# The four rotation products of a state-space scan block on VectorE instead of GpSimd

## The chip, the core and the metric

The kernel runs on one core of a Trainium2 chip. A core has engines that each work through a queue of their own in order: TensorE (PE; its weight loads are shown as PEld), VectorE (DVE), ScalarE (ACT), GpSimd (POOL), and SyncE (SP), which issues the DMA transfers. They work side by side and wait for one another through semaphores. The metric is the device time of one execution in microseconds (us); lower is better. For the kernel before there are three timed runs and one further execution under the profiler.

## The reference

Two layers of a hybrid block over 1024 latent and 256 context tokens of width 1024. Each layer makes one input projection whose columns go to three mixers, differential attention, a state-space scan in both directions (S5), and Fourier mixing, then an output projection and a squared-ReLU MLP. The change lies in the scan, which in the reference is

```
bu_re = jnp.einsum('blgp,gnp->blgn', uf, bb_re)
bu_im = jnp.einsum('blgp,gnp->blgn', uf, bb_im)
...
_, _, s_re, s_im = lax.associative_scan(_affine_combine, (a_re, a_im, bu_re, bu_im), axis=1)
...
y = einsum(s_re, c_re) - einsum(s_im, c_im)          # s5_readout
```

a complex linear recurrence s[t] = a s[t-1] + b u[t] for each of 16 groups with 64 states, in both directions, followed by a gelu and a gated unit (GLU).

## The kernel before

The scan is done over chunks of 8 tokens: 160 chunks for 1280 tokens, two groups at a time, so that a layer has 8 blocks. The complex rotation in the recurrence is taken out by multiplying with precomputed cosines and sines (the tile CS), so that a real scan with the magnitude rho remains, and is put back after it. A block of `states` thus runs, in this order:

- PE: transposes of the inputs (L997, L998), then the products with the block's matrices (L1005); ACT copies the result into VS (L1006 to L1008)
- four instructions of 128x640 float32 elements on POOL: T1 = VS cos, T2 = VS sin (L1012, L1013) ahead of the scan, T1 = Z cos, T2 = Z sin (L1020, L1021) behind it
- DVE: the sums of the first pair (L1014, L1015, 128x320), four scans (L1018, 128x160), the sums of the second pair, shifted by one chunk (L1027 to L1031)
- `readout`, one block later: PE multiplies the states with the output matrices (L1039, L1040, L1041), ACT and DVE make the gelu (L1044 to L1049), and after every fourth block SP writes eight transfers to HD (L1052)

There are 16 blocks in all, hence 64 such products.

The scan is not a stage of its own. It is a generator, `mixers`, of which `run` takes a step after each tile of the input projection. The projection (`in_proj`) multiplies 24 matmuls per tile of 128 tokens (L584; for the last column block, V, twice 12, L611). The weights of a column block are split into a rounded part and a rest by ACT and DVE (L159, L160) before PE can use them. A tile of queries or keys is then normalised and rotated in `qk_post` on DVE (L534 to L545); its inverse square root is a 128x8 power on POOL (L133), and PE transposes the result (L551).

What follows is attention: the loads of keys from KD (L633, tiles s_t) and of queries from QD (L641), the scores (L649), and, taken in steps between them, `glu`, which loads the scan's result from HD (L1076) and multiplies it on PE (L1085).

The order of instructions on each engine is not written out by hand. The tile framework simulates the program when it is built (`schedule_with_timeline_sim=True`) and fixes each queue by the times that it works out, so that a change of engine moves other instructions too. Tiles come from pools with a fixed number of buffers; the scan's work tiles are in `bg`, 7 buffers here, and PSUM has four banks for the projection and four for the rest.

Of the kernel before, what the change touches and what calls it, by code (L numbers as in the profile page):

```python
# [18 lines left out]
ALU = mybir.AluOpType  # L19
# [48 lines left out]
class Block:  # L68
# [890 lines left out]
    def ssm(self, l):  # L959
        nc, io = self.nc, self.io  # L960
        last = l == DEPTH - 1
        c0 = 32 if last else 0
        work = self.tl('kv', [128, 2, 8, NCH])
        HH = work[:, 0]
        ut = self.tl('kv', [128, 2560])
        U = ut[:, 0:2048].rearrange('c (j f) -> c j f', j=8)
        for h in range(2):
            nc.sync.dma_start(U[:, :, h * 128:h * 128 + 128],
                              self.UF[0:SEQ, h * 128:h * 128 + 128].rearrange('(c j) f -> c j f', j=8))

        def x1(i, part=128):
            return work[0:part, 1, 2 * i:2 * i + 2]

        def load(b):
            PA = self.tl('pa', [128, 2, 5, 128])
            nc.sync.dma_start(PA[:, :, 1:5], self.PD[l][b])
            kw = self.KW[l][b]
            for g in range(2):
                w = kw[:, g, 0:128]
                w = bass.AP(w.tensor, w.offset, [(SP, 8), *w.ap])  # L980
                nc.sync.dma_start(PA[:, g, 0], w)
            CS = self.bg([128, 2, 2, NCH])
            nc.sync.dma_start(CS, self.CD[l][b])
            return PA, CS

        def states(b, PA, CS):
            g0 = b * 2
            uc = ut[0:32, 2304:2560].rearrange('c (j f) -> c j f', j=8)
            nc.sync.dma_start(uc, self.UF[SEQ:TOK, g0 * 16:g0 * 16 + 32].rearrange('(j c) f -> c j f', c=32))
            UC = x1(2, 32)[:, :, 0:128]  # L990
            UM = ut[:, 2048:2304].rearrange('c (g f) -> c g f', g=2)
            for dst, src in ((UC, uc), (UM, U[:, :, g0 * 16:g0 * 16 + 32])):
                for g in range(2):
                    nc.scalar.copy(dst[:, g].rearrange('c (j q) -> c j q', j=8), src[:, :, g * 16:g * 16 + 16])
            p = self.pf((128, 2, NCH))
            for g in range(2):
                nc.tensor.transpose(p[:, g, 0:32], UC[:, g], self.idn[0:32, 0:32])  # L997
                nc.tensor.transpose(p[:, g, 32:160], UM[:, g], self.idn)  # L998
            UT = x1(b % 2)
            nc.scalar.copy(UT, p)  # L1000
            VS = self.bg([128, 2, 2, NCH])
            for g in range(2):
                p = self.pf((128, 2, NCH))
                for j in range(2):
                    nc.tensor.matmul(p[:, j], PA[:, g, 1 + j], UT[:, g], start=True, stop=True)  # L1005
                nc.scalar.copy(VS[0:64, :, g], p[0:64])  # L1006
                nc.scalar.copy(VS[64:128, :, g, 0:32], p[64:128, :, 0:32][:, :, ::-1])
                nc.scalar.copy(VS[64:128, :, g, 32:160], p[64:128, :, 32:160][:, :, ::-1])  # L1008
            cos = CS[:, 0].unsqueeze(1).to_broadcast([128, 2, 2, NCH])
            sin = CS[:, 1].unsqueeze(1).to_broadcast([128, 2, 2, NCH])  # L1010
            T1, T2, Z = (self.bg([128, 2, 2, NCH]) for _ in range(3))
            nc.gpsimd.tensor_tensor(T1, VS, cos, ALU.mult)  # L1012
            nc.gpsimd.tensor_tensor(T2, VS, sin, ALU.mult)  # L1013
            nc.vector.tensor_tensor(VS[:, 0], T1[:, 0], T2[:, 1], ALU.add)  # L1014
            nc.vector.tensor_tensor(VS[:, 1], T1[:, 1], T2[:, 0], ALU.subtract)  # L1015
            for j in range(2):
                for g in range(2):
                    nc.vector.tensor_tensor_scan(Z[:, j, g], self.rho[:, l * 16 + g0 + g:l * 16 + g0 + g + 1].to_broadcast([128, NCH]),  # L1018
                                                 VS[:, j, g], 0.0, ALU.mult, ALU.add)
            nc.gpsimd.tensor_tensor(T1, Z, cos, ALU.mult)  # L1020
            nc.gpsimd.tensor_tensor(T2, Z, sin, ALU.mult)  # L1021
            S = VS
            nc.vector.memset(S[0:64, :, :, 0:1], 0.0)
            nc.vector.memset(S[64:128, :, :, 31:32], 0.0)
            for j, op in enumerate((ALU.subtract, ALU.add)):
                a, c = T1[:, j], T2[:, 1 - j]
                nc.vector.tensor_tensor(S[0:64, j, :, 1:160], a[0:64, :, 0:159], c[0:64, :, 0:159], op)  # L1027
                if not last:
                    nc.vector.tensor_tensor(S[64:128, j, :, 0:31], a[64:128, :, 0:31][:, :, ::-1],
                                            c[64:128, :, 0:31][:, :, ::-1], op)  # L1030
                nc.vector.tensor_tensor(S[64:128, j, :, 32:160], a[64:128, :, 31:159][:, :, ::-1],  # L1031
                                        c[64:128, :, 31:159][:, :, ::-1], op)
            return PA, UT, S

        def readout(b, PA, UT, S):
            g0 = b * 2
            y = self.pf((128, 2, NCH))
            for g in range(2):
                nc.tensor.matmul(y[:, g, c0:], PA[:, g, 0], UT[:, g, c0:], start=True, stop=False)  # L1039
                nc.tensor.matmul(y[:, g, c0:], PA[:, g, 3], S[:, 0, g, c0:], start=False, stop=False)  # L1040
                nc.tensor.matmul(y[:, g, c0:], PA[:, g, 4], S[:, 1, g, c0:], start=False, stop=True)  # L1041
            yv = y[:, :, c0:]
            sq, y4 = (x1(2 + i)[:, :, c0:] for i in range(2))
            nc.scalar.activation(y4, yv, AF.Copy, scale=0.25)  # L1044
            nc.scalar.activation(sq, yv, AF.Square)
            nc.vector.tensor_scalar(sq, sq, 0.044715, 1.0, ALU.mult, ALU.add)
            nc.vector.tensor_tensor(sq, sq, y4, ALU.mult)
            nc.scalar.activation(sq, sq, AF.Tanh, scale=4.0 * math.sqrt(2.0 / math.pi))
            nc.vector.scalar_tensor_tensor(HH[:, g0 % 8:g0 % 8 + 2, c0:], sq, 1.0, y4, ALU.add, ALU.mult)  # L1049
            if b % 4 == 3:  # L1050
                for i in range(8):
                    nc.sync.dma_start(self.HD[b // 4 * 8:b // 4 * 8 + 8, :, i, c0:].rearrange('g q c -> q g c'),  # L1052
                                      HH[i * 16:i * 16 + 16, :, c0:])


        prev, nxt = None, load(0)
        yield
        for b in range(9):
            cur = (b, states(b, *nxt)) if b < 8 else None
            yield  # L1060
            if prev is not None:
                readout(prev[0], *prev[1])
            if b < 7:
                nxt = load(b + 1)
            if b:
                yield
            prev = cur
# [370 lines left out]
```

## Time and profile before

| | us |
|---|---|
| timed runs | 3080.57, 3086.21, 3086.28 |
| their median | 3086.21 |
| the profiled execution | 3082.04 |
| its span, first to last instruction | 3080.3 |
| PE busy in the span | 2948.4 (96%) |
| DVE busy | 1980.6 (64%) |
| ACT busy | 1074.5 (35%) |
| POOL busy | 590.7 (19%) |

The span is the time from the first to the last instruction of the profiled execution; 1.7 us lie around it. Busy times are unions over an engine's instructions. The shares are averages over stages: the blocks of the scan run from 268 to 440 us of the span in layer 0 and from 1890 to 2066 us in layer 1.

### The profile page before, as it was taken

Reading aid. Unit: us, or ns where it says so; the run is one execution under the profiler, and the core shown is the slowest. Engines: PE = TensorE matmul, PEld = TensorE weight load, DVE = VectorE, ACT = ScalarE, POOL = GpSimd, SP = SyncE. Lnnn points to the kernel's source line nnn. Section 1 sums busy time; section 2 is a strip of 40 time slices with the busy share of each in tenths; the row PEclk is TensorE's granted clock in tenths of the full one; section 3 lists DMA queues with packets and bytes.
Section 4 is the critical chain, followed back from the end, with each engine's and each line's share of the span. In section 5 each row is a group of like instructions: output and inputs, shape, how many; then the busy total and the mean of one; then the engine's idle time right before and its main releaser. Section 6 shows DMA issues by size and latency. Waiting matters only on the chain.

```text
span 3080.3 us, 41053 instructions
## 1 busy us (share of the span) xinstructions
PE 2948.4 (96%) x15309; PEld 2417.2 (78%) x15309; DVE 1980.6 (64%) x3546; ACT 1074.5 (35%) x2379; POOL 590.7 (19%) x515
## 2 busy tenths in 40 slices
PE   6899989999999999999999999989999999999999
PEld 3567777668888888888888877768889888888887
DVE  7867856666567677676545557959866555455444
ACT  5224436666331121121222243427864222211222
POOL 0644510000100000000266123526631000000000
PEclk9899999999999999999999999999999999999999
DMA  8345473435122232231222044571241111111111
GB/s 301 111 147 163 157 199 102 129 110 159 47 63 88 74 98 76 83 96 42 72 81 82 32 154 142 156 171 51 66 141 42 52 45 55 48 49 42 55 49 65
DMA packets 280852, 299.93 MB, mean 97 GB/s; under 512 B 47159, under 2 KB 191949, under 8 KB 280653
## 3 DMA queue, kind: packets, MB, share of 16 engines
q1 hardware_dynamic: 280652, 297.31, 31.8%
q8 instruction: 120, 1.97, 0.3%
q14 instruction: 80, 0.65, 0.1%
HBM read 229.31 MB, written 67.93 MB: 96 GB/s over the span
## 4 chain that ended last, share of the span: by engine, by line
PE 78%; DVE 8%; DMA 4%; issue 2%; ACT 2%; POOL 1%; SPq 0%; DVEq 0%; POOLq 0%; ACTq 0%
PE b_t L1241 26%; PE b_t L1264 25%; PE b_t L1208 7%; PE b_t L584 4%; PE b_t L695 4%; PE s_t L649 3%; PE b_t L417 2%; PE b_t L611 2%; PE b_t L691 1%; DVE mx L663 1%; DMA qs_t<-QD 1%; DMA s_t<-KD 1%; PE f_t L1124 1%; ACT s_t L665 1%; PE b_t L649 1%
## 5 line engine op out<-in xcount | busy, mean ns | idle before, releaser
L1264 PE MATMUL b_t<-hid_t,w_t 128*128 128x512 f32 (+1 forms) x3840 | 809.2, 370 | 0.0
L1241 PE MATMUL b_t<-s_t,w_t 128*128 128x512 f32 (+1 forms) x3840 | 800.4, 369 | 0.0
L1264 PEld LDWEIGHTS b_t<-hid_t,w_t 128*128 128x128 f32 x3840 | 669.7, 189 | 121.7 <-issue 1.9
L1241 PEld LDWEIGHTS b_t<-s_t,w_t 128*128 128x128 f32 x3840 | 669.1, 189 | 121.2 <-issue 1.1
L1266 DVE SCALAR_TENSOR_TENSOR kv_t<-b_t,mod,kv_t 128x512 f32<-128x512 f32 (+1 forms) x640 | 439.5, 694 | 240.2 <-PE b_t L1264 239.6
L159 ACT CAST w_t<-r_t 128x512 fp32r<-128x512 f32 x336 | 194.8, 619 | 797.3 <-PE b_t L1264 528.9
L584 PE MATMUL b_t<-w_t,s_t 128*128 128x512 f32 (+1 forms) x1392 | 356.7, 411 | 17.9 <-ACT s_t L474 6.0
L160 DVE TENSOR_TENSOR w_t<-r_t,w_t 128x512 fp32r<-128x512 f32 x328 | 230.8, 732 | 208.1 <-ACT w_t L159 207.7
L584 PEld LDWEIGHTS b_t<-w_t,s_t 128*128 128x128 f32 x1392 | 266.7, 198 | 81.7 <-issue 6.8
L133 POOL TENSOR_TENSOR sm<-sm,mhalf 128x8 f32<-128x8 f32 (+3 forms) x66 | 104.0, 1575 | 598.3 <-DVE sm L702 234.0
L1245 DVE TENSOR_TENSOR t_t<-b_t,t_t 128x512 f32<-128x512 f32 x160 | 101.3, 633 | 143.3 <-ACT t_t L1244 143.1
L892 POOL TENSOR_TENSOR bg_t<-pt_t,bw_t 128x256 f32<-128x256 f32 x56 | 42.8, 765 | 740.2 <-DMA bw_t<-BD 662.3
L695 PE MATMUL b_t<-kv_t,kv_t 128*128 128x128 f32 x1312 | 178.8, 281 | 3.0 <-ACT kv_t L692 2.8
L695 PEld LDWEIGHTS b_t<-kv_t,kv_t 128*128 128x128 f32 x1312 | 164.7, 194 | 16.7 <-issue 7.8
L663 DVE TENSOR_REDUCE mx<-s_t 128x1 f32<-128x1024 f32 x128 | 155.0, 1219 | 29.7 <-PE s_t L649 29.1
L1244 ACT ACTIVATE t_t<-b_t 128x512 f32<-128x512 f32 x160 | 88.4, 552 | 216.2 <-PE b_t L1241 216.2
L159 ACT CAST hid_t<-t_t 128x512 fp32r<-128x512 f32 x160 | 92.4, 578 | 204.1 <-DVE t_t L1245 204.0
L665 ACT ACTIVATE s_t<-s_t,mx 128x1024 f32<-128x1024 f32 x128 | 143.7, 1123 | 38.0 <-DVE mx L664 31.1
L160 DVE TENSOR_TENSOR hid_t<-t_t,hid_t 128x512 fp32r<-128x512 f32 x160 | 106.7, 667 | 66.2 <-ACT hid_t L159 66.2
L378 DVE SCALAR_TENSOR_TENSOR ac_t<-bg_t,vc,ac_t 128x512 f32<-128x512 f32 x168 | 118.9, 744 | 33.8 <-DMA bg_t<-in_w_mod_dram 33.6
L649 PE MATMUL s_t<-s_t,qs_t 128*128 128x512 f32 x448 | 128.2, 412 | 8.5 <-ACT s_t L665 5.5
L611 PE MATMUL b_t<-w_t,s_t 128*128 128x512 f32 x480 | 115.8, 395 | 6.6 <-DVE w_t L160 3.4
(332 smaller groups left out, 3550.5 us busy)
## 6 DMA issues: line engine op xcount, KB each, us to landing
r_t<-in_w_ff_dram SPq DMA_DIRECT2D x256, 256.0 KB
bg_t<-in_w_mod_dram SPq DMA_DIRECT2D x96, 256.0 KB
r_t<-in_w_in_dram SPq DMA_DIRECT2D x64, 256.0 KB
qs_t<-QD SPq DMA_DIRECT2D x64, 256.0 KB
XD<-kv_t SPq DMA_DIRECT2D x16, 640.0 KB
KD<-t_t SPq DMA_DIRECT2D x40, 256.0 KB
s_t<-KD SPq DMA_DIRECT2D x32, 320.0 KB
QD<-t_t SPq DMA_DIRECT2D x36, 256.0 KB
```

What stands on the lines that cost most here:

```text
L159: self.nc.scalar.copy(h, raw)
L160: (eng or self.nc.vector).tensor_tensor(l, raw, h, ALU.subtract)
L584: nc.tensor.matmul(p[:, :cols], a[:, ts], W[k][:, b, :cols], start=(n == 0), stop=(n == 23))
L611: nc.tensor.matmul(p, a[:, ts], W[k][:, b], start=(n == 0), stop=(n == 11))
L649: nc.tensor.matmul(dst, QS[e][:, m, h], ST[h][m][:, a:b], start=(e == 0), stop=(e == 1))
L663: nc.vector.tensor_reduce(mx[:, m, 1:2], S, AX.X, ALU.max, negate=True)
L665: nc.scalar.activation(PR[m][:, 0:SEQ], S, AF.Exp, bias=mx[:, m, 0:1], accum_out=sm[:, m, 1:2])
L695: nc.tensor.matmul(o, WT[:, kt * 128:(kt + 1) * 128], V[kt // 5][:, kt % 5, h * 128:(h + 1) * 128], start=(c == 0), stop=(c == len(ks) - 1))
L1208: nc.tensor.matmul(p[:, :w], W[c][a][:, k], b[k][:, s:s + w], start=(n == 0), stop=(n == 23))
L1241: nc.tensor.matmul(p[:, :w], W[a][:, k], b[k][:, s:s + w], start=(q == 0), stop=(q == 23))
L1264: nc.tensor.matmul(p[:, :w], W[a][:, cs], hid[b][:, s:s + w], start=(q == 0), stop=(q == n - 1))
L1266: nc.vector.scalar_tensor_tensor(xs, p[:, :w], self.mod[l][:, 40 + c, g // 2:g // 2 + 1], xs, ALU.mult, ALU.add)
```

## The change

The four products of a block are issued to DVE instead of POOL. Nothing else in the source differs, and the line numbers stay.

```
             T1, T2, Z = (self.bg([128, 2, 2, NCH]) for _ in range(3))
-            nc.gpsimd.tensor_tensor(T1, VS, cos, ALU.mult)
-            nc.gpsimd.tensor_tensor(T2, VS, sin, ALU.mult)
+            nc.vector.tensor_tensor(T1, VS, cos, ALU.mult)
+            nc.vector.tensor_tensor(T2, VS, sin, ALU.mult)
...
-            nc.gpsimd.tensor_tensor(T1, Z, cos, ALU.mult)
-            nc.gpsimd.tensor_tensor(T2, Z, sin, ALU.mult)
+            nc.vector.tensor_tensor(T1, Z, cos, ALU.mult)
+            nc.vector.tensor_tensor(T2, Z, sin, ALU.mult)
```

POOL loses 64 instructions and DVE gains 64, and the simulated order of PE, DVE, ACT and SP changes around them. First DVE, in the first scan block of layer 0; sm, t_t and qk_t belong to `qk_post`, w_t to the weights of the next column block, bg_t to the scan.

```order
 L535 TENSOR_SCALAR sm_2459<-sm_2459 128x8
+L1012 TENSOR_TENSOR bg_t_2408<-bg_t_2395,bg_t_2334 128x640
+L1013 TENSOR_TENSOR bg_t_2409<-bg_t_2395,bg_t_2334 128x640
 L160 TENSOR_TENSOR t_t_2472<-b_t_2466,t_t_2471 128x512
 L160 TENSOR_TENSOR w_t_2545<-r_t_2543,w_t_2545 128x512
 L545 TENSOR_TENSOR qk_t_2454<-qk_t_2454,sm_2460 128x512
+L1014 TENSOR_TENSOR bg_t_2395<-bg_t_2408,bg_t_2409 128x320
+L1015 TENSOR_TENSOR bg_t_2395<-bg_t_2408,bg_t_2409 128x320
 L160 TENSOR_TENSOR w_t_2550<-r_t_2548,w_t_2550 128x512
 L160 TENSOR_TENSOR w_t_2555<-r_t_2553,w_t_2555 128x512
-L1014 TENSOR_TENSOR bg_t_2395<-bg_t_2408,bg_t_2409 128x320
-L1015 TENSOR_TENSOR bg_t_2395<-bg_t_2408,bg_t_2409 128x320
```

The two products stand in DVE's queue ahead of a weight split, and the sums that use them two weight splits earlier than before.

Then PE at the end of layer 1's projection, where the last block's readout (f_t_17823) stands among the matmuls of V (L611). Before:

```order
 L611 MATMUL b_t_17915<-w_t_17495,s_t_6605 128x512
 L611 MATMUL b_t_17915<-w_t_17495,s_t_6609 128x512
-L1040 MATMUL f_t_17823<-bg_t_17694,pa_t_17648 128x128
 L611 MATMUL b_t_17915<-w_t_17495,s_t_6605 128x512
 L611 MATMUL b_t_17915<-w_t_17500,s_t_6606 128x512
-L1041 MATMUL f_t_17823<-bg_t_17694,pa_t_17648 128x128
-L1039 MATMUL f_t_17823<-kv_t_16510,pa_t_17648 128x128
-L1040 MATMUL f_t_17823<-bg_t_17694,pa_t_17648 128x128
-L1041 MATMUL f_t_17823<-bg_t_17694,pa_t_17648 128x128
```

and now, behind the last matmul of V (b_t_17943) and ahead of the first scores (L649):

```order
 L611 MATMUL b_t_17943<-w_t_17510,s_t_6612 128x512
 L611 MATMUL b_t_17943<-w_t_17510,s_t_6608 128x512
+L1040 MATMUL f_t_17823<-bg_t_17694,pa_t_17648 128x128
+L1041 MATMUL f_t_17823<-bg_t_17694,pa_t_17648 128x128
+L1039 MATMUL f_t_17823<-kv_t_16510,pa_t_17648 128x128
+L1040 MATMUL f_t_17823<-bg_t_17694,pa_t_17648 128x128
+L1041 MATMUL f_t_17823<-bg_t_17694,pa_t_17648 128x128
+L649 MATMUL s_t_18042<-s_t_17987,w_t_17993 128x512
+L649 MATMUL s_t_18042<-s_t_17987,w_t_17994 128x512
```

The readout has moved 32 matmuls of V back, to the very end of the projection. Between it and the GLU product that needs the second half of HD (L1085) there were 32 L611, 16 L649 and two L1085 on PE; now there are 32 L649 and two L1085. In layer 0 the same readout moved 12 matmuls back, 19 L611 instead of 31 follow it, and four more L649 stand ahead of that L1085.

Last SP's queue in layer 1, where the last block's matrices (pa_t, from PD and KW) and its cosines (bg_t, from CD) are loaded; s_t are the key loads for attention.

```order
 L633 DMA s_t_17999<-KD 64x1280 x2
-L633 DMA s_t_18000<-KD 64x1280 x2
+L633 DMA s_t_18000<-KD 64x1280
+L976 DMA pa_t_17648<-PD_178 128x2x512
+L981 DMA pa_t_17648<-KW_180 128x1x128 x2
+L633 DMA s_t_18000<-KD 64x1280
+L983 DMA bg_t_17652<-CD_188 128x640
```

These four loads stood ahead of all key loads and now stand behind seven of them and four query loads.

## Rows read from the trace of the kernel before

**Rows 1.** Stretches: PE, PEld, DVE, ACT, POOL busy us (instructions), PE clock, DMA.

```profile
280.00:360.00 80.00, 68.85 (x331) 55.74 (x329) 71.56 (x126) 34.21 (x84) 46.18 (x25) 0.96 0.38 123
1900.00:2000.00 100.00, 90.43 (x442) 73.94 (x441) 93.38 (x156) 45.27 (x115) 55.12 (x31) 0.95 0.47 145
```

**Rows 2.** PE groups, 262 to 440 us: busy us, mean ns | idle before, releasers.

```profile
L611 PE MATMUL b_t<-w_t,s_t 128*128 128x512 f32 x240 | 58.0, 396 | 3.3 <-DVE w_t L160 1.7 <-DVE t_t L160 1.6
...
L551 PE MATMUL b_t<-idn,qk_t 128*128 128x128 f32 x52 | 8.3, 273 | 1.4 <-DVE qk_t L545 1.4
L1041 PE MATMUL f_t<-bg_t,pa_t 128*128 128x160 f32 x32 | 8.0, 336 | 1.3 <-DVE bg_t L1031 1.3
L1040 PE MATMUL f_t<-bg_t,pa_t 128*128 128x160 f32 x32 | 7.9, 332 | 4.8 <-DVE bg_t L1031 4.8
```

**Rows 3.** PE groups, 1890 to 2066 us.

```profile
L611 PE MATMUL b_t<-w_t,s_t 128*128 128x512 f32 x240 | 57.8, 395 | 3.3 <-DVE w_t L160 1.7 <-DVE t_t L160 1.6
...
L1041 PE MATMUL f_t<-bg_t,pa_t 128*128 128x128 f32 x32 | 7.3, 313 | 2.5 <-DVE bg_t L1031 2.4
```

**Rows 4.** Timeline of DVE, layer 0: start us, us, instruction.

```profile
306.28 0.69 DVE L542 TENSOR_TENSOR qk_t<-qk_t,t_t 128x512 f32<-128x512 f32 x1
...
331.38 0.69 DVE L545 TENSOR_TENSOR qk_t<-qk_t,sm 128x512 f32<-128x512 f32 x1
331.99 0.69 DVE L539 TENSOR_TENSOR qk_t<-t_t,rt_t 128x512 f32<-128x512 f32 x1
...
336.07 2.04 DVE L545 TENSOR_TENSOR qk_t<-qk_t,sm 128x512 f32<-128x512 f32 x1 [0.80 <-POOL sm L133]
...
341.19 0.48 DVE L1014 TENSOR_TENSOR bg_t<-bg_t,bg_t 128x320 f32<-128x320 f32 x1
341.60 0.48 DVE L1015 TENSOR_TENSOR bg_t<-bg_t,bg_t 128x320 f32<-128x320 f32 x1
...
422.86 0.33 DVE L1046 TENSOR_SCALAR kv_t<-kv_t 128x320 f32<-128x320 f32 x1 [2.62 <-ACT kv_t L1045]
423.23 0.49 DVE L1047 TENSOR_TENSOR kv_t<-kv_t 128x320 f32<-128x320 f32 x1
```

**Rows 5.** Timeline of POOL, layer 0.

```profile
305.79 1.94 POOL L133 TENSOR_TENSOR sm<-sm,mhalf 128x8 f32<-128x8 f32 x1 [4.29 <-DVE sm L535]
...
336.01 1.55 POOL L1012 TENSOR_TENSOR bg_t<-bg_t,bg_t 128x640 f32<-128x640 f32 x1
```

**Rows 6.** DVE groups, 268 to 422 us.

```profile
L545 DVE TENSOR_TENSOR qk_t<-qk_t,sm 128x512 f32<-128x512 f32 x11 | 12.8, 1160 | 3.4 <-POOL sm L133 3.1
...
L1047 DVE TENSOR_TENSOR kv_t<-kv_t 128x320 f32<-128x320 f32 x7 | 9.2, 1315 | 0.2
...
L1046 DVE TENSOR_SCALAR kv_t<-kv_t 128x320 f32<-128x320 f32 x7 | 7.0, 996 | 8.4 <-ACT kv_t L1045 8.4
```

**Rows 7.** DVE groups, 1890 to 2048 us.

```profile
L160 DVE TENSOR_TENSOR w_t<-r_t,w_t 128x512 fp32r<-128x512 f32 x16 | 14.8, 953 | 0.4 <-ACT w_t L159 0.3
...
L1046 DVE TENSOR_SCALAR kv_t<-kv_t 128x256 f32<-128x256 f32 x8 | 10.3, 1282 | 9.0 <-ACT kv_t L1045 9.0
...
L1047 DVE TENSOR_TENSOR kv_t<-kv_t 128x256 f32<-128x256 f32 x8 | 8.4, 1046 | 0.2
```

**Rows 8.** Timeline of PE at the end of layer 0's and layer 1's projection.

```profile
440.88 3.78 PE L1085 MATMUL b_t<-kv_t,w_t 128*128 128x512 f32 x4 [7.29 <-DMA kv_t<-HD]
...
2046.63 7.51 PE L611 MATMUL b_t<-w_t,s_t 128*128 128x512 f32 x32
...
2056.25 2.38 PE L649 MATMUL s_t<-s_t,w_t 128*128 128x512 f32 x8
2067.67 3.69 PE L1085 MATMUL b_t<-kv_t,w_t 128*128 128x512 f32 x4 [9.03 <-DMA kv_t<-HD]
```

**Rows 9.** The chain that ended last, layer 0: start us, us, what.

```profile
422.71 9.89 DMA qs_t<-QD
```

**Rows 10.** POOL groups, 268 to 422 us.

```profile
L133 POOL TENSOR_TENSOR sm<-sm,mhalf 128x8 f32<-128x8 f32 x11 | 21.9, 1991 | 30.7 <-DVE sm L535 30.6
```

## The prediction

> **What bounds the kernel now.** I looked first at the busy times by stretch, for the two places where the scan blocks lie, in their densest part [rows 1]. PE is busy 68.9 of 80 us in layer 0 and 90.4 of 100 us in layer 1, DVE 71.6 and 93.4. So two engines are nearly full there. Neither leads by much, and a change of DVE's work can show in the time, which the 64% of the whole span would not suggest. Elsewhere the change touches nothing: the products exist only in these blocks.
>
> Second, PE's own groups, since PE sets the end of the kernel: only what PE waits for in these stretches can be won. In layer 0 it waits 1.3 and 4.8 us for the scan's last sums (L1031), 3.3 us for weights and context halves split on DVE (L160), 1.4 us for a rotated key tile (L545) [rows 2]; in layer 1 2.4 us for L1031 and 3.3 us for L160 [rows 3]. That is 8.5 us for the scan and 8.0 us for DVE's other work. Third, the ends of both stages: PE stands still 7.3 us and 9.0 us ahead of the GLU product, which waits for the last block's result to go to memory and back [rows 8].
>
> **What the change takes from DVE and what it adds.** The timelines of DVE and POOL show why the products are no free work where they are. At 336.07 a multiplication L545 takes 2.04 us, while POOL's L1012 runs from 336.01 for 1.55 us; the same instruction takes 0.69 us at 331.38, when POOL has no product [rows 4, 5]. A DVE instruction with two inputs that starts under a product is thus held until about the product's end, 1.35 us here. How much this is in all I read from DVE's groups. In layer 0 eleven L545 have a mean of 1.160 instead of 0.69 us, seven L1047 1.315 instead of 0.49, seven L1046 0.996 instead of 0.33 [rows 4, 6]: 11 x 0.47 + 7 x 0.825 + 7 x 0.666 = 15.7 us. In layer 1 eight L1046 have 1.282, eight L1047 1.046 and sixteen weight splits 0.953 [rows 7]; against the same undisturbed 0.33, 0.49 and 0.69 us this is 7.6 + 4.4 + 4.2 = 16.2 us. These groups alone hold 31.9 us of DVE time, 0.50 us for each of the 64 products.
>
> Added are 64 instructions of 128x640 with two inputs. The trace has no such instruction on DVE. Two neighbours of 320 elements start 0.41 us apart, two of 512 elements 0.61 us apart [rows 4], which is 0.20 us for 192 elements; 640 elements take 0.41 + 320 x 0.20 / 192 = 0.74 us of the queue, 64 of them 47.4 us. The balance for DVE lies between two ends: +15.5 us if only the groups above shrink, and 47.4 - 64 x 1.35 = -39 us if every product held an instruction as long as the one at 336.07. I take 0, since the groups above give the better part of it and the smaller ones, which I have not counted, should shrink too. So DVE stays as full as it is, and its cover, PE at 86 and 90% of these stretches, stays as it is.
>
> What does change is the block's own chain. Two pairs of products on POOL take 4 x 1.55 us [rows 5] with a handover to DVE each time; on DVE they take 4 x 0.74 = 3.0 us. The sums L1031 come more than 3 us earlier per block, and PE's queue now has most readouts further back. So I let 7 of the 8.5 us of waits for L1031 go (they can be no shorter than 0, and at worst all stay). Of the 8.0 us of waits for weight splits and key tiles I let half go, 4 us: the stretched instructions that stood ahead of them are short again, but products now stand ahead of some of them in the same queue, as at the first block's weight split. Bounds: 0 and 8.0 us. What the weight splits delay is PE itself; what L545 delays are the transposes and with them the buffers of the next tile.
>
> **Moved work.** In layer 1 the last readout comes 32 matmuls of V later, and they took 7.5 us [rows 8]. If the result's way through memory starts from the readout, the waiting L1085 comes 7.3 us later relative to the end of the projection; 16 more score matmuls stand ahead of it, worth about 3.8 us (eight took 2.38), leaving +3.5. If the way is set by the transfers queued before it, keys and queries, the later readout costs nothing and the score matmuls are won: -3.8 us. If the score matmuls find no free PSUM tile, +7.3. In layer 1 the last block's loads also fell behind seven key loads, which speaks for the first. I take +3. In layer 0 the readout moves by 12 matmuls, 2.7 us, but there the chain shows a query load landing at 432.6 us as what released the last of the writes to HD [rows 9], so I let the later place cost nothing and count the four extra score matmuls, -0.9 us; at worst it is +1.8.
>
> The sum: -7 - 4 + 3 - 0.9 = -9 us. The profiled execution took 3082.0 us, so its like would take 3073. The median of the runs shown is 4.2 us above that execution, and the four times of this kernel lie between 3080.6 and 3086.3 with their middle at 3084.1; from there I forecast **3075 us**.
>
> **A rule against the trace.** Under a power L133 from 305.79 for 1.94 us, the multiplication L542 takes its usual 0.69 us at 306.28 [rows 4, 5]: the powers that stay on POOL hold nothing. By this row the new DVE instructions run free beside them, and the balance above stands. The Trainium skill, page "SBUF — State Buffer", section "Who interferes with whom", says that VectorE instructions with two SBUF inputs and GpSimd instructions that read SBUF exclude each other, whichever starts second being blocked for the whole of the other. The trace agrees for the products and not for the powers. What it would do here: in layer 0 eleven powers fill 21.9 of 154 us, 14% [rows 10]; 14% of 64 new instructions would each be held about 1 us, 9 us in all, which would use up the gain.
>
> **Rivals.** *The tails take it back* (0.22): the waits in the blocks go, -11 us, but layer 1's readout costs +7.3 and layer 0's +1.8, and the PE clock falls during the longer waits. 3082 to 3084 us. For it: the readout now stands behind all of V. Against: score matmuls that can run are put into that hole.
>
> *The waits only change hands* (0.09): PE's waits for L1031 vanish, but PE comes to the next tile earlier and waits there for key tiles and weights that are no earlier, since DVE has as much to do. 3083 us, no change. For it: DVE is at 89 and 93% in these stretches.
>
> *DVE becomes the bound* (0.16), the other side: what is stretched today is partly time in which DVE would have waited anyway, so it does not come back. The place is the dense part of both layers. There DVE has 8.4 and 6.6 us to spare [rows 1] and gets 16 and 20 products, 11.8 and 14.8 us; the excess, 3.4 + 8.2 = 11.6 us, is then PE's, and weight splits queue behind products. 3096 us. It decides when less than 11.6 / 36 = 0.32 us per product comes back, against the 0.50 us counted above.
>
> *The rule holds for powers too* (0.03): 9 us more on DVE, 3084 us, by the trace unlikely.
>
> **How the numbers follow.** My forecast has 0.50, with its own range 3063 (all 16.5 us of waits go and both ends win, 3084 - 21) to 3080. Within 0.2%, 6.2 us, about what a measurement of this kernel can tell from no change, lie the tails, the exchanged waits and the rule: 0.34, of which I give 0.03 to slower for tails at their worst. Slower: 0.16 + 0.03. The range that leaves out the slower cases is 3063 to 3093.
>
> **What would show it.** Right: DVE's L545, L1047 and L1046 near 0.69, 0.49 and 0.33 us; the products near 0.85 us each and 0.74 us apart; PE's idle for L1031 near zero; DVE busy in the dense parts about as now. Wrong: DVE above 95% there and PE waiting longer for L160 or L545 than 8 us in all; or L1085 in layer 1 waiting 13 us or more. What would make the whole wrong is a product on DVE of 1 us or more, or a readout on the last block that starts late because its loads land late.

## The result, and the profile after

Six timed runs of the changed kernel have a median of 3070.75 us (3064.47 to 3071.39), six of the kernel before, taken beside them, 3086.1 us. The ratio is 0.9948 with a 95% interval of 0.9935 to 0.9961, so the change makes the kernel 16 us faster (12 to 20). A later set of runs gave 0.9940 (0.9928 to 0.9952). The profiled execution took 3066.24 us, 15.8 us less than that of before, with a span of 3064.4 us.

The two dense stretches come first, as in [rows 1]; the columns are those.

```profile
280.00:360.00 80.00, 73.25 (x357) 60.81 (x355) 73.05 (x158) 37.03 (x90) 20.49 (x9) 0.94 0.45 139
1900.00:2000.00 100.00, 94.51 (x479) 77.83 (x478) 92.53 (x192) 49.38 (x125) 22.42 (x10) 1.00 0.55 163
```

DVE is as full as before (73.1 and 92.5 us instead of 71.6 and 93.4) although it now does the products; PE gets 26 and 37 more matmuls through in the same time. Its granted clock in layer 1 is 1.00 instead of 0.95, but in layer 0 it is 0.94 instead of 0.96.

DVE's groups from 268 to 422 us answer to [rows 6]: busy us, mean ns | idle before.

```profile
L545 DVE TENSOR_TENSOR qk_t<-qk_t,sm 128x512 f32<-128x512 f32 x12 | 8.2, 681 | 1.6 <-POOL sm L133 1.6
...
L1012 DVE TENSOR_TENSOR bg_t<-bg_t,bg_t 128x640 f32<-128x640 f32 x8 | 6.6, 824 | 16.1 <-ACT bg_t L1008 16.0
...
L1047 DVE TENSOR_TENSOR kv_t<-kv_t 128x320 f32<-128x320 f32 x8 | 3.9, 482 | 0.1
...
L1046 DVE TENSOR_SCALAR kv_t<-kv_t 128x320 f32<-128x320 f32 x8 | 2.5, 318 | 2.6 <-ACT kv_t L1045 2.6
```

The three groups that had means of 1.160, 1.315 and 0.996 us are back at 0.681, 0.482 and 0.318 us. What DVE now stands and waits for is the input of the products, ScalarE's copy L1008. In layer 1, from 1890 to 2048 us, L1046 and L1047 answer to [rows 7], where they had 1.282 and 1.046 us:

```profile
L1047 DVE TENSOR_TENSOR kv_t<-kv_t 128x256 f32<-128x256 f32 x8 | 3.3, 415 | 0.0
L1046 DVE TENSOR_SCALAR kv_t<-kv_t 128x256 f32<-128x256 f32 x8 | 2.3, 288 | 1.1 <-ACT kv_t L1045 1.1
```

PE's groups, first from 262 to 440 us [rows 2], then two of layer 1 from 1890 to 2066 us [rows 3].

```profile
L611 PE MATMUL b_t<-w_t,s_t 128*128 128x512 f32 x240 | 58.2, 396 | 0.0
...
L1041 PE MATMUL f_t<-bg_t,pa_t 128*128 128x160 f32 x32 | 7.1, 302 | 0.0
...
L997 PE MATMUL f_t<-idn,kv_t 32*128 32x32 f32 x16 | 4.0, 251 | 6.8 <-ACT kv_t L994 6.8
```

```profile
L611 PE MATMUL b_t<-w_t,s_t 128*128 128x512 f32 x240 | 56.9, 393 | 0.0
...
L1041 PE MATMUL f_t<-bg_t,pa_t 128*128 128x128 f32 x32 | 6.2, 275 | 0.0
```

Every wait for L1031, L160 and L545 is gone, and one has grown: in layer 0 L997 waits 6.8 us for the copy L994, where it waited 2.2 us before.

To account for the whole difference I cut both traces at the same matmuls: a scan stretch runs from the last Fourier product to the last matmul of V, and the stretch behind it to the last matmul of the output projection. The kernel before:

```profile
259.58:429.10 169.52, 156.49 (x761) 128.26 (x760) 129.81 (x243) 68.86 (x174) 77.33 (x44) 0.98 0.62 177
429.10:848.16 419.06, 396.20 (x2277) 303.55 (x2277) 266.84 (x508) 236.36 (x589) 35.43 (x31) 0.98 0.39 114
1868.43:2054.14 185.71, 175.63 (x854) 144.71 (x854) 143.51 (x253) 72.32 (x190) 81.72 (x47) 0.97 0.60 167
2054.14:2370.26 316.12, 294.51 (x1986) 262.45 (x1985) 235.21 (x448) 207.30 (x517) 140.71 (x92) 0.97 0.30 83
```

and the changed one:

```profile
262.81:424.33 161.52, 154.77 (x761) 128.66 (x760) 126.64 (x275) 69.49 (x174) 25.61 (x12) 0.97 0.65 182
424.33:844.49 420.16, 396.17 (x2278) 303.41 (x2277) 267.76 (x508) 235.91 (x589) 35.40 (x31) 0.98 0.40 115
1863.25:2037.96 174.71, 169.22 (x844) 139.71 (x844) 136.41 (x282) 71.70 (x187) 31.55 (x15) 1.00 0.64 171
2037.96:2354.36 316.40, 295.59 (x1996) 262.87 (x1995) 233.69 (x451) 208.71 (x520) 139.38 (x92) 0.98 0.32 87
```

The scan stretches are 8.0 and 11.0 us shorter, the stretches behind them 1.1 and 0.3 us longer, together -17.6 us; the rest of the kernel, which the change does not touch, is 1.7 us longer. Length less PE's busy time is PE's idle time: 13.0 to 6.8, 22.9 to 24.0, 10.1 to 5.5 and 21.6 to 20.8 us, in all -10.5 us. The other 7.1 us are busy time that PE needs less. About 5 of them are clock in layer 1: 100 us at 0.95 [rows 1] against 100 us at 1.00. In the trace before, the granted clock is 0.50, the lower level of 1.2 GHz, from 1925 to 1927, 1939 to 1941 and 1969 to 1972 us, each time behind a wait of PE, of 2.4 us for L1031, 1.8 for L1000 and 1.9 for L994. In layer 0 the clock goes the other way, 80 us at 0.94 instead of 0.96, which takes back 1.6 us. The remaining 4 us I cannot assign.

### The profile page after: what moved, and what is told of

The parts are those of the page before. It is cut to its first block, busy times and chain, and to the rows that moved or that the text cites. A ratio compares the mean times of both kernels' runs of the same rounds, so it can differ in the third digit from the quotient of the medians.

```text
span 3064.4 us, 41016 instructions
## 1 busy us (share of the span) xinstructions
PE 2939.7 (96%) x15309; PEld 2411.4 (79%) x15309; DVE 1972.0 (64%) x3610; ACT 1075.4 (35%) x2379; POOL 486.8 (16%) x451
## 4 chain that ended last, share of the span: by engine, by line
PE 84%; DVE 7%; DMA 5%; ACT 2%; issue 1%; POOL 1%; SPq 1%; DVEq 0%; ACTq 0%; POOLq 0%
PE b_t L1241 26%; PE b_t L1264 25%; PE b_t L584 7%; PE b_t L1208 7%; PE b_t L695 4%; PE s_t L649 3%; PE b_t L611 2%; PE b_t L691 2%; PE b_t L417 2%; PE f_t L1124 1%; DMA qs_t<-QD 1%; PE b_t L649 1%; DMA kv_t<-HD 1%; DVE mx L663 1%; DMA s_t<-KD 1%
## 5 line engine op out<-in xcount | busy, mean ns | idle before, releaser
L160 DVE TENSOR_TENSOR w_t<-r_t,w_t 128x512 fp32r<-128x512 f32 x328 | 226.2, 718 | 218.7 <-ACT w_t L159 217.9
L133 POOL TENSOR_TENSOR sm<-sm,mhalf 128x8 f32<-128x8 f32 (+3 forms) x66 | 109.4, 1657 | 735.5 <-DVE sm L535 278.6
L695 PEld LDWEIGHTS b_t<-kv_t,kv_t 128*128 128x128 f32 x1312 | 164.3, 194 | 15.8 <-issue 6.9
L159 ACT CAST hid_t<-t_t 128x512 fp32r<-128x512 f32 x160 | 92.5, 578 | 206.6 <-DVE t_t L1245 206.5
L160 DVE TENSOR_TENSOR hid_t<-t_t,hid_t 128x512 fp32r<-128x512 f32 x160 | 107.4, 671 | 66.2 <-ACT hid_t L159 66.2
L649 PE MATMUL s_t<-s_t,qs_t 128*128 128x512 f32 x448 | 127.6, 410 | 7.4 <-ACT s_t L665 4.4
L611 PE MATMUL b_t<-w_t,s_t 128*128 128x512 f32 x480 | 115.2, 395 | 0.0
```

Of the source, the lines that this page charges most:

```text
L159: self.nc.scalar.copy(h, raw)
L160: (eng or self.nc.vector).tensor_tensor(l, raw, h, ALU.subtract)
L611: nc.tensor.matmul(p, a[:, ts], W[k][:, b], start=(n == 0), stop=(n == 11))
L649: nc.tensor.matmul(dst, QS[e][:, m, h], ST[h][m][:, a:b], start=(e == 0), stop=(e == 1))
L695: nc.tensor.matmul(o, WT[:, kt * 128:(kt + 1) * 128], V[kt // 5][:, kt % 5, h * 128:(h + 1) * 128], start=(c == 0), stop=(c == len(ks) - 1))
```

## The experiments

Theory A: products on POOL take DVE's time, because they hold its two-input instructions (and L1046, which has one input), and DVE's time is nearly the bound in the scan stretches. Rival B: what counted is the block's chain, in which DVE handed the work to POOL and waited for it (16.1 us of waits for L1021 in the two scan stretches before, 8.8 and 7.3). Rival C: only the order of the queues or the clock changed luckily. All ratios are to the kernel before, timed on the same chip; its medians there were 3082.4 us for the first four runs, 3081.9 for the next and 3084.3 for the last.

| run | median us | ratio (95% interval) | DVE busy us |
|---|---|---|---|
| products again on GpSimd beside (e3) | 3117.24 | 1.0113 (1.0099 to 1.0127) | 2041.6 |
| products twice (e4) | 3101.97 | 1.0064 (1.0050 to 1.0077) | 2017.6 |
| second pair alone (e6) | 3085.26 | 1.0009 (1.0000 to 1.0018) | 1983.7 |
| kernel before | | 1 | 1980.6 |
| layer 0 alone (e1) | 3074.57 | 0.9974 (0.9963 to 0.9984) | 1979.2 |
| own buffer for UC (e8) | 3074.92 | 0.9974 (0.9964 to 0.9983) | 1973.6 |
| layer 1 alone (e2) | 3071.38 | 0.9967 (0.9954 to 0.9979) | 1972.0 |
| first pair alone (e5) | 3072.03 | 0.9965 (0.9951 to 0.9979) | 1968.8 |
| the changed kernel | 3070.75 | 0.9948 (0.9935 to 0.9961) | 1972.0 |
| trip to GpSimd kept (e10) | 3065.06 | 0.9942 (0.9929 to 0.9955) | 1972.2 |
| the changed kernel again (e9) | 3065.03 | 0.9940 (0.9928 to 0.9952) | 1971.8 |
| HD written from GpSimd's queue (e11) | 3061.63 | 0.9934 (0.9922 to 0.9946) | 1972.0 |
| one instruction less in the gelu (e12) | 3053.34 | 0.9903 (0.9890 to 0.9916) | 1969.1 |
| no products at all (e7) | 3046.08 | 0.9884 (0.9870 to 0.9897) | 1928.4 |

**One layer at a time.**

```
-            nc.vector.tensor_tensor(T1, VS, cos, ALU.mult)
+            (nc.gpsimd if l else nc.vector).tensor_tensor(T1, VS, cos, ALU.mult)
```

and so for all four products; the second run has the engines the other way round.

> Only layer 0's 32 products go to VectorE; layer 1 keeps them on GpSimd. My theory is that the gain is local to each layer: layer 0's stretch lost 6.9 us in the profile, so this gives about 3079 us (3077 to 3082), with the waits for L1031, L160 and L545 gone in layer 0 and there as before in layer 1. Rival 1, the gain is all layer 1's (clock): 3086. Rival 2, the 2.9 us that the profile lost between the layers belong to layer 0's new order: 3076.

> Only layer 1's 32 products go to VectorE. My theory: layer 1's stretch lost 10.7 us, about half of it as waits and half as clock that is no longer taken away, so about 3075 us (3073 to 3078), and the granted clock between 1900 and 2000 us at 1.00 instead of 0.95. Rival, the clock of layer 1 was chance: 3080 to 3081.

Layer 0 alone is worth 0.26% or 8.0 us, layer 1 alone 0.33% or 10.2 us; the sum, 18.2, is the 16 to 18.5 us of both. The scan stretch of the changed layer takes 161.3 and 179.2 us, that of the other 186.0 and 170.1, as before. So the gain is local, and rival 1 falls for layer 0; its rival 2 is too near to be told apart by the time, but the 2.9 us between the layers are gone in the profiles of both runs, so layer 0's order is not what moves them. In layer 1 the stretch is 4.5 us longer than in the changed kernel, with 0.95 of the clock between 1900 and 2000 us in place of the 1.00 that I had expected: kernels that do the same work in that layer keep different shares of the clock. The kernel before has 0.95 there too, so layer 1's gain of 10.2 us came without the clock, and that run's rival, a clock that was chance, falls as the whole cause.

**Products on GpSimd beside, which nobody waits for.** The changed kernel with 64 further products on POOL:

```
-        with self.scope(pa=2):
+        with self.scope(pa=2, sh=1):
...
-        def states(b, PA, CS):
+        def states(b, PA, CS, SH=self.tl('sh', [128, 2, 2, NCH])):
...
+            nc.gpsimd.tensor_tensor(SH, cos, sin, ALU.mult)      # behind each product
```

> The changed kernel with a further 64 products of 128x640 on GpSimd, cosine times sine into a tile that nobody reads: GpSimd is as busy as before, with the same access to memory, but no engine waits for it, and the queues of PE, VectorE, ScalarE and SyncE are those of the changed kernel. Theory 1, most of the gain is VectorE time that the products on GpSimd stretched: VectorE instructions are held again by 20 us or more in each layer, the waits for L1031, L160 and L545 come back, and the time returns to about 3085 us (3080 to 3092; it can be worse than before, since VectorE also has its own products). Theory 2, the gain is the shorter chain of a block (no handover to GpSimd and back) and the new order: the stretched instructions cost nothing and the time stays at 3069 to 3074.

The kernel is 51 us slower than the changed one (1.0113 against 0.9948 of 3085), more than I had expected and 35 us slower than before. The scan stretches of this run:

```profile
259.34:443.52 184.18, 161.76 (x761) 132.20 (x760) 159.71 (x275) 69.73 (x174) 81.89 (x44) 0.94 0.56 158
1885.68:2086.91 201.23, 179.36 (x842) 146.01 (x841) 169.06 (x274) 72.06 (x187) 88.62 (x47) 0.95 0.56 150
```

Against the changed kernel DVE is busy 33.1 and 32.7 us longer with no instruction more, and the stretches are 22.7 and 26.5 us longer: 49 us of time for 66 us of DVE, 0.75. PE's idle time is 22.4 and 21.9 us, with the waits for L160, L545 and L1031 back and those of L997 for L994 at 9.6 and 9.0 us; 17 of the 49 us are busy time of PE, for the same matmuls at 0.94 and 0.95 of the clock instead of 0.97 and 1.00. The run's timeline of POOL and of DVE at one place, start us, us, instruction:

```profile
301.15 1.66 POOL L1020 TENSOR_TENSOR sh_t<-bg_t 128x640 f32<-128x640 f32 x1
302.89 1.73 POOL L1021 TENSOR_TENSOR sh_t<-bg_t 128x640 f32<-128x640 f32 x1
```

```profile
301.43 1.46 DVE L1029 TENSOR_TENSOR bg_t<-bg_t,bg_t 64x62 f32<-64x62 f32 x1
302.81 0.42 DVE L1031 TENSOR_TENSOR bg_t<-bg_t,bg_t 64x256 f32<-64x256 f32 x1
303.24 1.72 DVE L1027 TENSOR_TENSOR bg_t<-bg_t,bg_t 64x318 f32<-64x318 f32 x1
304.98 0.22 DVE L1029 TENSOR_TENSOR bg_t<-bg_t,bg_t 64x62 f32<-64x62 f32 x1
```

A subtraction of 62 elements takes 0.22 us beside an idle POOL and 1.46 us under a product, whose end it waits for. No queue of PE, ScalarE or SyncE differs from the changed kernel's and nobody waits for these products, so neither B nor C can explain the loss: the products' use of POOL beside DVE costs this much alone, and theory A's mechanism is shown. (The powers L133 queue behind the products on POOL, but DVE waits for them 5.9 us instead of 4.8, too little to matter.) It does not follow that the 16 us of the change are its return, because there DVE pays for most of the time that it gets back, as the runs below show. The Trainium skill, page "SBUF — State Buffer", section "Who interferes with whom", says that a VectorE instruction with two SBUF inputs shuts out a GpSimd instruction that reads SBUF, or is shut out by it, and that a reduction never is. The trace agrees: the subtraction that came second waits for the product's end, and L534, a reduction, has a mean of 0.670 us in this run's layer 0, as without products; one that starts at 299.60, under a product that runs from 299.29 for 1.79 us, takes 0.68 us.

**Each product twice on VectorE.**

```
+            nc.vector.tensor_tensor(SH, VS, cos, ALU.mult)       # behind each product, with its own inputs
```

> The changed kernel with each product done twice on VectorE, the second into a tile that nobody reads: 64 more instructions, 47 us more VectorE time, nothing on GpSimd. Theory 1, VectorE is nearly the bound in the dense parts: it has 7.0 of 80 and 7.5 of 100 us to spare there and gets about 16 and 20 further products, 11.8 and 14.8 us; the excess of 12 us comes out as time: 3083 us (3078 to 3090). Theory 2, VectorE has cover enough and only the order of its queue matters: 3071 to 3075. Theory 3, VectorE is the bound throughout: 3071 + 47 = 3118.

Neither: 3102 us lies between theories 1 and 3. DVE's busy time is 45.6 us longer than in the changed kernel, the span 35.6 us: 0.78 us for 1 us of DVE. The spare time that I read from the dense stretches as cover (7.0 and 7.5 us) is not cover; most of it stands where DVE waits for others, and is not there to be filled. A later DVE shows up as later transposes: PE waits 5.4 and 6.7 us for L545 in the two scan stretches, where the changed kernel has none.

**One pair of the two.** The other two products go back to GpSimd.

> Only the first pair (L1012, L1013, ahead of the scan) goes to VectorE; the second pair stays on GpSimd. By VectorE's books: the first pair stretched 27.4 of the 44.4 us counted under products before, and costs 23.7 us on VectorE, net -3.7; the wait of VectorE for L1021, 16.1 us in both layers, stays. At the price that the doubled products showed (0.66 us of time for 1 us of VectorE) this gives -2.4 us, 3082 where before has 3084 (3079 to 3085). Rival, each pair brings half of the gain, because what counts is the shorter chain and the order: -8 us, 3076.

> Only the second pair (L1020, L1021, behind the scan) goes to VectorE; the first stays on GpSimd. Books: 16.5 us of stretch and 16.1 us of waiting for L1021 go, 23.7 us of products come, net -8.9 us of VectorE time, by 0.66 this is -6 us: 3078 where before has 3084 (3075 to 3081). Rival, halves: 3076; rival, only all four products together bring anything, since one product left on GpSimd still holds what starts under it: 3084.

Both expectations miss, and in opposite directions: the first pair alone brings 10.8 us, the second alone costs 2.8 us or nothing, together they bring 16 to 18.5. The books of the expectations were too low. Their 44.4 us come out when an instruction's undisturbed time is taken from the shorter ones of its own kind in the trace before, where some groups are held almost throughout: all eight L1046 of layer 1 together have a mean of 1.282 us [rows 7], and 0.288 in the changed kernel. Counted against the medians of the changed kernel (every DVE instruction over 0.15 us longer, from 260 to 400 and from 1880 to 2050 us) there are 52.4 us of stretch before, 35.1 of them under the first pair; 19.5 are left with the first pair moved and 31.6 with the second moved. So 32.9 us go with the first pair and 20.8 with the second, each for 23.7 us of products by the forecast's figure, and DVE's busy time follows: 11.8 us less with the first, 3.1 more with the second, 8.6 less with both. This gives the order of the two, not the sizes: from the first pair alone to the changed kernel DVE gets 3.2 us busier, and yet the ratio falls from 0.9965 to 0.9948 and 0.9940, 5 to 8 us, about as much as the intervals can tell apart.

**No products.** The sums read VS and Z; the rotation is left out.

```
-            T1, T2, Z = (self.bg([128, 2, 2, NCH]) for _ in range(3))
+            Z = self.bg([128, 2, 2, NCH])
+            T1 = T2 = VS          # ahead of the first sums; T1 = T2 = Z ahead of the second
```

> The four products of a block are left out (the sums read VS and Z instead of T1 and T2), so neither VectorE nor GpSimd has them: the floor of what any placement of them can give. Theory 1, VectorE is the bound of the scan's stretches at 0.66 us of time for 1 us of VectorE: 47.4 us less gives 31 us, 3039 to 3045. Theory 2, PE is the bound as soon as its waits are gone: after the change PE waits 6.8 and 5.5 us in the blocks and about 9 and 11 us at the ends, and at most the waits in the blocks and what they cost in clock can still be won: 3052 to 3062.

3046.08 us is a hair above theory 1's range and below theory 2's. Against the changed kernel's profile DVE has 43.6 us less and the span is 20.6 us shorter, 0.47 for 1, because PE runs out of waits: in the scan stretches it is idle 0.8 and 3.6 us, with the clock at 1.00. So DVE is nearly the bound going up, and PE takes over soon going down.

**A trip to GpSimd for each pair.**

```
             nc.vector.tensor_tensor(T2, VS, sin, ALU.mult)
+            nc.gpsimd.tensor_scalar(T1[:, 0, 0, 0:1], T1[:, 0, 0, 0:1], 1.0, None, ALU.mult)
...
             nc.vector.tensor_tensor(T2, Z, sin, ALU.mult)
+            nc.gpsimd.tensor_scalar(T1[:, 0, 0, 0:1], T1[:, 0, 0, 0:1], 1.0, None, ALU.mult)
```

> The changed kernel with a tiny GpSimd instruction (one element of each partition of T1, times one) behind each pair of products on VectorE, so that the sums of the pair wait for a trip to GpSimd and back, as before, but nothing is held on VectorE; the queues of PE, VectorE, ScalarE and SyncE are those of the changed kernel. Theory 1, a good part of the gain was that VectorE no longer stands and waits for GpSimd (16.1 us for L1021 before): the waits come back, 32 trips of 0.3 to 2 us, and at 0.4 to 0.75 us of time for 1 us of VectorE the kernel is 5 to 12 us slower than the changed one, 3076 to 3083. Theory 2, only the stretch counted, since other VectorE work stands between a pair and its sums: within 3 us of the changed kernel.

> The changed kernel once more, as the base for the three runs beside it: ratio 0.993 to 0.996 to the kernel before. Its second profile also shows what differs between two executions of the same program: the 1.9 us at the start, the 2.9 us between the layers and the half clock there should come out otherwise, the scan's stretches (161.5 and 174.7 us) the same within 1 us.

3065.06 against 3065.03 us beside it: the trips cost nothing that intervals of 4 us to either side can show, theory 2. The tiny instruction takes 0.57 to 0.68 us on POOL (means of the two lines in layer 0), and DVE mostly has other work between a pair and its sums. The 16.1 us in which DVE waited for L1021 were therefore not the price of the trip itself. What this run does not copy is the length of the old chain: two products on POOL took 3.4 us by the means of their groups in layer 0, where two on DVE take 1.5.

The second profile of the changed kernel shows what two executions of one program differ by: its scan stretches are 161.9 and 177.1 us, the latter 2.4 us off the first profile where I had expected 1 at most, its span 3063.8. The 2.4 us in layer 1 are clock, 0.98 instead of 1.00, so of the 5 us won there at least half comes and goes. The stretch between the layers, from the last matmul of layer 0's output projection to the last of its MLP, takes 921.8 us as in the first profile, against my expectation; over all profiles here it takes 921.8 to 924.7 us with the same work, and what moves it stays open.

**Three attempts at a better kernel**, each on the changed one. The first gives UC a buffer of its own. In the changed kernel PE waits 6.75 us ahead of L997 at 300.37 because the copy L994 overwrites a slot that the gelu of the block before still reads:

```profile
299.49 0.49 DVE L1049 SCALAR_TENSOR_TENSOR kv_t<-kv_t 128x320 f32<-128x320 f32 x1
```

```profile
300.02 0.50 ACT L994 COPY kv_t<-kv_t 32x128 f32<-32x128 f32 x2 [2.35 <-DVE kv_t L1049]
```

```profile
300.37 0.31 PE L997 MATMUL f_t<-idn,kv_t 32*128 32x32 f32 x1 [6.75 <-ACT kv_t L994]
```

```
-            UC = x1(2, 32)[:, :, 0:128]
+            UC = self.tl('uc', [128, 2, 128])[0:32]
```

> The changed kernel with a buffer of its own for UC, the block's transposed context input, which shares a slot with the gelu's square of the block before. In the changed kernel PE waits 6.75 us at 300 us for the copy L994, which waits for the gelu's last step on VectorE (L1049 at 299.49), and the granted clock falls to 0.66 to 0.83 behind it. Theory: this wait goes, the readouts stand 80 to 100 matmuls further ahead in PE's queue, and the ends of the projection find HD written: 10 to 15 us less than the changed kernel, 3055 to 3061. Rival: VectorE is as full as before, so the waits only move to L1031 or L545: 3066 to 3072.

The wait goes, and PE waits 6.5 us for the next block's matrices (PD) instead, 6.0 of them at one place. The last readout of layer 1 ends 13.2 us earlier than the changed kernel's, and the GLU product still waits 10.1 us for HD, because the write then stands behind key and query loads (12.4 and 9.4 us in the chain of work there). At 0.9974 it is slower than the changed kernel: worse than the theory and than the rival.

The second writes HD from POOL's queue:

```
-                    nc.sync.dma_start(self.HD[b // 4 * 8:b // 4 * 8 + 8, :, i, c0:].rearrange('g q c -> q g c'),
+                    nc.gpsimd.dma_start(self.HD[b // 4 * 8:b // 4 * 8 + 8, :, i, c0:].rearrange('g q c -> q g c'),
```

> The changed kernel with the eight writes to HD after every fourth block issued from GpSimd's queue instead of SyncE's, where they stand behind five to eight query loads and take 8.2 us to issue. Theory 1, SyncE's queue sets when HD is there: the waits of L1085, 4.4 and 7.6 us, shrink by half or more, 3062 to 3067. Theory 2, the DMA engines are full at the end of the projection (share 1.05), and whichever queue issues, the data come no sooner: 3068 to 3074.

3061.63 beside 3065.03 us, with intervals that overlap: inconclusive by the time. By the trace theory 1 holds in layer 1, where the eight writes take 4.2 instead of 8.2 us to issue and L1085 waits for nothing at its second half, and theory 2 in layer 0, where the read of HD stays behind eight query loads on SyncE, lands at 439.8 us, and the wait is 7.4 us. The order moved as well: layer 0's scan stretch is 5.3 us longer than the changed kernel's, with a new wait of 4.9 us for L545.

The third takes one DVE instruction from each gelu:

```
-            nc.scalar.activation(sq, yv, AF.Square)
-            nc.vector.tensor_scalar(sq, sq, 0.044715, 1.0, ALU.mult, ALU.add)
-            nc.vector.tensor_tensor(sq, sq, y4, ALU.mult)
+            nc.scalar.activation(sq, yv, AF.Square, scale=math.sqrt(0.044715))
+            nc.vector.scalar_tensor_tensor(sq, sq, 1.0, y4, ALU.add, ALU.mult)
```

> The changed kernel with one VectorE instruction fewer in each readout: the square is scaled on ScalarE, and L1046 (times 0.044715, plus 1) goes into the multiplication L1047. This takes 16 instructions of 0.24 us start to start, about 4 us, from VectorE, and one trip between engines from each gelu. Theory 1, VectorE time is worth 0.4 to 0.75 us of time for 1 us: 2 to 3 us less than the changed kernel beside it. Theory 2, the order moves as well and is worth more than 3 us in either direction, as with the buffer for UC.

It is the fastest kernel of the study: 0.9903, 11.7 us less than the changed one beside it, where DVE's own 2.7 us would give 2. Theory 2, then: the order moves as well. Against the changed kernel's first profile the wait for L994 at the first block is 2.5 instead of 6.8 us (the gelu's chain is shorter), the scan stretches are 2.6 and 0.4 us shorter, and the stretches behind them 3.7 and 7.2 us, with the last readouts 10.5 instead of 4.3 us ahead of the end of V in layer 0 and 0.7 us ahead instead of 1.1 behind in layer 1. The profiled execution is this kernel's fastest, 4.4 us under its median, so these stretches show more than the 11.7 us. Which part is the gelu's chain and which is the order I did not separate.

## Why the prediction was right

The forecast was 3075 us, the time is 3070.75, within the forecast's own range of 3063 to 3080, and the mechanism that it names, stretch that comes back and pays for the products, is in the profiles. The size of the change is another matter: 9 us were forecast, from 3084.1, and 16 (12 to 20) were measured, from 3086.1. That the time lies only 4 us under the forecast is in part luck: the base came out 2 us higher, and terms that the sum left out, of either sign, cancel in part. By its steps, against the profiles:

- *DVE's balance, 0.* A product takes 0.82 us, and two start 0.74 us apart, as worked out from the smaller instructions:

```profile
286.79 0.82 DVE L1012 TENSOR_TENSOR bg_t<-bg_t,bg_t 128x640 f32<-128x640 f32 x1
287.53 0.82 DVE L1013 TENSOR_TENSOR bg_t<-bg_t,bg_t 128x640 f32<-128x640 f32 x1
288.38 0.49 DVE L1014 TENSOR_TENSOR bg_t<-bg_t,bg_t 128x320 f32<-128x320 f32 x1
```

The groups that I counted fell to the values named. Over the kernel DVE's busy time fell by 8.6 us, 1980.6 to 1972.0. The zero was a guess between two ends; both its terms were off, in the same direction. The stretch that went is 52.4 us, 0.82 for each product instead of 0.50 (15.7 in the forecast's first sum should be 15.6), and the products cost 43.6 us by the run without them instead of 47.4, which makes -8.8. At 0.47 to 0.78 us for 1 us of DVE this is 4 to 7 of the 16 us.
- *Waits for L1031, -7.* All went, -8.5.
- *Waits for L160 and L545, -4.* Under-sized: all went, -8.0. I had let half stay because products stand ahead of weight splits in DVE's queue; they do, and cost nothing there.
- *The end of layer 1, +3.* Half the size: from the end of V to the waiting L1085 PE's waits went from 9.0 to 10.6 us, +1.5 (7.6 and 1.2 us of L1085 and 1.8 us of L649 for the softmax). The branch that I took is the one that the trace shows: the writes to HD start to issue as the last step of the readout's gelu, L1049, ends.

```profile
2043.86 0.41 DVE L1049 SCALAR_TENSOR_TENSOR kv_t<-kv_t 128x256 f32<-128x256 f32 x1
```

```profile
2044.29 8.19 SPq L1052 DMA_DIRECT2D HD<-kv_t  x8
```

From the last readout's end to the waiting L1085 it is 19.4 us, and was 20.8; from the end of V it is 20.5 instead of 13.5, 7.0 us later where 7.3 were worked out, and PE is busy 5.5 us more in it. The other branch has a part too, since the writes take 8.2 us to issue behind query loads. The chain of work there:

```profile
2042.85 9.20 DMA qs_t<-QD
2052.04 0.02 issue
2052.06 2.06 DMA HD<-kv_t
2054.12 0.02 issue
2054.14 4.31 DMA kv_t<-HD
2058.45 0.04 issue
2058.49 3.78 PE b_t L1085 x4
```

- *The end of layer 0, -0.9.* It came out at the bound, +1.8: 4.4 us for HD, 1.8 us for the GLU's weights and 2.9 us for a softmax make 9.1 instead of 7.3. The later readout did count (20.2 us from its end to L1085, before 18.9), and the extra score matmuls waited themselves for PSUM tiles that the softmax frees. Behind the ends PE waits 3.0 us less in the rest of attention, so that both stretches together add 0.3 us.
- *Not in the sum: waits that take their place.* PE's waits for ScalarE's copies in the scan stretches rose by 5.7 us, from 6.5 to 12.2, most of it at L997 in layer 0, 2.2 to 6.8. This is the rival in which waits change hands; it took a third of what the blocks gave.
- *Not in the sum: the clock.* Some 5 us in layer 1, of which half went again in the changed kernel's second profile, less 1.6 us in layer 0. I had used it only in a rival, as a loss. It is the term that was missing, and with the waits for L160 and L545 it makes up for the exchanged ones, in part by chance.
- *The rival that DVE becomes the bound* was wrong on the return, 52.4 us of stretch or 0.82 us per product against its threshold of 0.32, and nearly right on the price: where DVE does get fuller, in the two runs that load it, each microsecond costs 0.75 to 0.78, without the spare time that the rival first let be filled.
- *The rule for powers*: DVE's instructions under a power alone are not longer in any trace where I counted them, so that rival falls.

What stays open: DVE's busy time, at its price, gives 4 to 7 of the 16 us. For the remaining 9 to 12 there are the shorter chain of a block (3.4 us for a pair on POOL, 1.5 on DVE), the order that follows from it, and the clock. Two comparisons speak for such a part: layer 0 alone gains 8.0 us with 1.4 us less of DVE, and the second pair on top of the first gains 5 to 8 us with 3.2 us more. The runs show that the trip itself costs nothing measurable and that a shorter gelu also gives more than its DVE time, but they do not separate the three, so rivals B and C stand for this part.

## What to carry to other kernels

An operation that is moved off a full engine may still use that engine's time: look at the neighbours' durations while it runs, not only at the shares, and count their excess over the same instruction elsewhere. Moving a part of such work can fail where moving all of it pays: count for each part what it holds against what it costs on the other engine, and take an instruction's undisturbed time from a run in which nothing holds it. And where the order of the queues follows from the engines chosen, a few microseconds of one engine's time move the readouts and loads around it, so price a change by a run that leaves the order alone as well as by the sum.

## What was not expected of the hardware

Some powers on POOL get longer, and why is open. L133, a power of 8 elements with a median of 1.95 us, takes 3.42 us where it starts 0.4 us ahead of two products on DVE (L1020 at 293.43, L1021 at 294.17):

```profile
293.06 3.42 POOL L133 TENSOR_TENSOR sm<-sm,mhalf 128x8 f32<-128x8 f32 x1 [18.14 <-DVE sm L535]
```

The difference is that of two products on DVE, 2 x 0.74 us, and in the run with each product twice powers with three such products behind their start take 4.15 us, about 3 x 0.74 more. Of the 38 powers of 128x8, none is over 2.4 us in the kernel before and five in the changed one, up to 3.75, as far as the records of POOL's spans go. But two of the five have no product on DVE beside them, five others with a product beside them stay at 2.21 us or less, and one takes 3.75 us in the kernel without products. So a product on DVE may hold a power, but what decides it is not shown. No DVE instruction beside a power alone is longer. The Trainium skill's rule of the page named above, that the one that comes second waits for the whole of the other, is thus seen in full for the products, 1.46 us for an instruction of 0.22. The powers do not follow it: the long ones started first, and DVE's instructions under them are not held.
